# Hybrid trunk kernel: the loads of kept weight sums move to their place in the order of use

## The chip, the cores and the metric

The kernel runs on one NeuronCore of one Trainium2 chip. The metric is the device time of one execution in microseconds. Of three runs of the kernel before, the median is 1556.36 us, the lowest 1554.48 us and the highest 1556.77 us.

## The reference, cut to what matters

A decoder trunk of two layers works on 256 tokens of width 1024, all in float32. Each layer is a feed-forward block (FFN), a token mixer, and another FFN, so there are four FFNs; they are numbered 1 to 4 here, in order of time.

```python
def swiglu(x, w_in, w_out):
    gate, up = jnp.split(x @ w_in, 2, axis=-1)
    return (jax.nn.silu(gate) * up) @ w_out
...
    for l in range(DEPTH):
        h = h + 0.5 * swiglu(rms_norm(h, ffn1_norm[l]), ffn1_w_in[l], ffn1_w_out[l])
        u = rms_norm(h, mix_norm[l])
        ...
        h = h + merged @ w_out[l]
        h = h + 0.5 * swiglu(rms_norm(h, ffn2_norm[l]), ffn2_w_in[l], ffn2_w_out[l])
    return rms_norm(h, final_norm)
```

`w_in` of an FFN is 1024 x 5632 and `w_out` 2816 x 1024. The mixer (a state-space branch and a delta-rule branch) has its own large projections and runs between FFN 1 and 2, and between FFN 3 and 4.

## The kernel before, in words

**The weight stream.** All large weights come from one DRAM tensor, `wst`, cut into tiles of 128 x 1024 float32 (512 KB). A tile goes through three steps. `load` (L167) issues its DMA on SyncE's queue into one of five buffers `wraw` (`NRAW`). `prep` (L180) splits it in two: ScalarE writes the rounded half `whi`, VectorE the remainder `wlo = wraw - whi`; there are five buffers of each (`NSPL`). Then TensorE multiplies with both halves (three matmuls for one product: high by high, and the two cross terms). `take` (L206) is called by the consumer; it issues loads and splits ahead, five splits ahead of the consumer, and loads as far as the five buffers go.

**The FFN's plan.** The string `FFN` gives the order of an FFN's steps: `f` is the first token chunk (4 tiles), `c` a chunk of the input projection (2 tiles, `chan_chunk`), `A` and `B` are the two parts of a block product of the output projection, and `d` is one plain tile of the output projection:

```python
FFN = "f" + 8 * "c" + "A" + 4 * "c" + "A" + 4 * "c" + "A" + 2 * "c" + "A" + 2 * "c" + "BdBBBddddd"
```

Four pairs of output tiles are multiplied by a scheme with seven products in place of eight, which needs sums of weight blocks. Four of the products stand in `A` (the PSUM tiles `p`), three in `B` (the PSUM tiles `o`).

**The kept sum.** For each `A`/`B` pair one tile, named `wsum` in the profile, lives from before `A` until its `B`. There are four slots for it, `y0` to `y3`, each used once in an FFN (the mixer uses the same slots for other tiles). It is filled by a plain load of one block on SyncE's queue (kind `"y"` in `load`), and then a second block is added to it by an accumulating DMA on GpSimd's queue (kind `"+"`, `add_to`, L165), which waits until the first has landed. `plan_ffn` puts both into the stream two `c` steps ahead of their `A`. In `A`, `prep` splits the sum (step `q1`); VectorE adds one raw tile onto another (tile `wraw<-wraw` in the profile) and one raw tile onto the sum; step `q3` splits the sum again, and then `add_to` adds a third block by another accumulating DMA. Step `q6` in `B` splits it for the last time. So an FFN has four plain loads of `wsum` and eight accumulating DMAs.

**What sets the order.** The kernel is traced in program order and a scheduler then orders each engine's queue by priority and by what it believes is ready. `tc.issue_after(ins)` ties the instructions traced inside its block behind `ins` on the queue of `ins`; it adds no semaphore. A load into `wraw` needs a buffer that is given back by the splits, so it stays near its place in the stream. A load into a slot `y` needs only that the slot is free. SyncE's queue also carries the norm vectors `nw` (`norm_vec`, L216, tied behind the last load), the mixer's small parameters and its DRAM round trips. GpSimd's queue carries the accumulating DMAs, four accumulating DMAs onto `h` in each FFN (`join`, L421), and the small powers `zz` of the norms (L214).

**The end of an FFN.** After the last `B` come five `d` tiles, the residual `h`, the norm (`rms_chain`), and the first chunk of what follows. Each queue runs in its own order, and a queue whose head waits holds what stands behind it.

Of the kernel before, what the change touches and what calls it, by code (L numbers as in the profile page):

```python
# [52 lines left out]
def trunk_kernel(ctx, tc, x, wst, wsm, norms, lpar, rpar, cst, out):  # L53
    nc = tc.nc
# [103 lines left out]
    state = {"loaded": 0, "prepped": 0, "taken": 0, "last": None, "hold": False, "behind": {}, "late": {}, "first": 0}  # L158
    raws, halves = {}, {}

    def tile_of(i):
        return wst[i // 2, :, (i % 2) * 1024 :][:, 0:1024]

    def add_to(r, i):
        G.dma_start(out=r[:], in_=tile_of(i), accum_op=ALU.add)  # L165

    def load(j):  # L167
        kind, i = stream[j][:2]
        if kind == "+":
            add_to(raws[stream[j][2]], i)  # L170
            return
        if kind == "y":
            r = slots.tile([P, 1024], F32, tag=f"y{state['first']}", name="wsum")
            state["first"] = (state["first"] + 1) % 4
        else:
            r = wpool.tile([P, 1024], F32, tag="wraw", name="wraw", bufs=NRAW)
        state["last"] = nc.sync.dma_start(r[:], tile_of(i))
        raws[j] = r

    def prep(i):  # L180
# [25 lines left out]
    def take():  # L206
        j = state["taken"]
        state["taken"] = j + 1
        ahead("loaded", limit[min(j + NSPL, n_forms) - 1], load)
        ahead("prepped", min(j + 1 if state["hold"] else j + NSPL, n_forms), prep)  # L210
        return halves.pop(j)
# [15 lines left out]
    for t in range(2):  # L227
        for n in range(2):
            nc.sync.dma_start(
                h[:, t, n * 512 : (n + 1) * 512], x[t * P : (t + 1) * P, n * 512 : (n + 1) * 512]  # L230
            )
        if t == 0:
            nc.sync.dma_start(cs[:, 0:P], cst[:, 0:P])
            ahead("loaded", 4, load)
# [30 lines left out]
    def rstd_of(t):  # L265

        ss = small([P, 2], "ss")
        for n in range(2):
            junk = tmp2("junk")
            state["square"] = act(junk[:], h[:, t, n * 512 : (n + 1) * 512], AF.Square, scale=1.0 / 32.0, accum_out=ss[:, n : n + 1])  # L270
        z = small([P, 2], "zz")
        ts(z[:, 0:1], ss[:, 0:1], ss[:, 1:2], ALU.add, EPS, ALU.add)
        rsqrt(z[:, 1:2], z[:, 0:1], [P, 1])
        return z[:, 1:2]
# [978 lines left out]
    for t in range(2):  # L1253
# [5 lines left out]
        r = rstd_of(t)  # L1259
# [137 lines left out]
```

## Time and profile before

| what | value |
|---|---|
| median of three runs | 1556.36 us |
| profiled execution, its own time | 1555.2 us |
| its span, first to last instruction | 1553.4 us |
| mean granted TensorE clock | 0.997 |
| TensorE busy (matmul) | 1529.5 us, 98% |
| VectorE busy | 1210.0 us, 78% |
| ScalarE busy | 945.9 us, 61% |
| bytes moved by DMA | 322.50 MB, mean 208 GB/s |
| loads of `wsum` on SyncE's queue | 16 of 512 KB |
| accumulating DMAs onto `wsum` on GpSimd's queue | 32 of 512 KB |
| loads of `wraw` | 520 of 512 KB |

In the profile, PE is TensorE's matmuls, PEld its weight loads, DVE is VectorE, ACT is ScalarE, POOL is GpSimd, and SPq is SyncE's queue. A row of the timeline gives the start and the duration in us, the engine, the line, the operation, what it writes and reads, and in brackets the idle time of the engine before it with what ended that. A row of the stretches gives from and to, the length, then for each engine busy time and instructions, then the granted TensorE clock, the mean busy share of the 16 DMA engines, and GB/s. A matmul's duration is modelled and overlaps the next one; the step from start to start is its rate.

### The profile page before, as it was taken

The numbers are of one execution on the slowest core, as the hardware profiler recorded it, in microseconds if no ns is written. First come the engines' busy times: TensorE is split into PE (matmuls) and PEld (weight loads), VectorE is DVE, ScalarE is ACT, GpSimd is POOL, SyncE is SP. The second block draws the span as 40 slices with busy tenths as digits, with TensorE's granted clock in tenths as the row PEclk, the third lists the DMA queues.
The fourth block names the chain that finished last, engine by engine and source line by source line (L and its number), as shares of the span: only waits on it lengthen the run. The fifth ranks groups of instructions, "written<-read, shape, count | busy, mean of one in ns | idle before, by whom it ended". The sixth has DMA issues, their size and how long they took to land.

```text
span 1553.4 us, 29029 instructions
## 1 busy us (share of the span) xinstructions
PE 1529.5 (98%) x11458; PEld 1384.0 (89%) x11458; DVE 1210.0 (78%) x1840; ACT 945.9 (61%) x1534; POOL 100.7 (6%) x108
## 2 busy tenths in 40 slices
PE   8999999999999999999899999999999999999998
PEld 7999889999888888999689998899998888889996
DVE  6778768967899766878677787699579996677786
ACT  5555677765576545655455566676756665455564
POOL 0000110000000000000100011000000000000010
PEclk9999999999999999999999999999999999999999
DMA  8878775653564686678967787666446557856785
GB/s 292 262 244 261 229 224 165 190 158 109 192 202 163 212 239 200 180 241 248 313 199 209 219 258 231 206 187 187 124 126 213 178 165 223 245 179 199 226 250 156
DMA packets 103439, 322.50 MB, mean 208 GB/s; under 512 B 23350, under 2 KB 24326, under 8 KB 102279
## 3 DMA queue, kind: packets, MB, share of 16 engines
q1 hardware_dynamic: 96390, 299.68, 58.4%
q0 software_dynamic: 6912, 20.97, 8.0%
q8 instruction: 90, 1.47, 0.4%
q14 instruction: 47, 0.38, 0.1%
HBM read 314.50 MB, written 1.92 MB: 204 GB/s over the span
## 4 chain that ended last, share of the span: by engine, by line
PE 82%; DVE 6%; DMA 4%; issue 3%; ACT 3%; POOL 1%; SPq 0%; POOLq 0%; ACTq 0%; DVEq 0%
PE fc L332 9%; PE fc L326 9%; PE fc L331 9%; PE t L321 3%; PE t L322 3%; PE t L323 3%; DMA wraw<-in_wst_dram 3%; PE b L323 3%; PE b L321 3%; PE b L322 3%; PE o L323 2%; PE o L322 2%; PE o L321 2%; DVE wlo L70 2%; PE p L322 2%
## 5 line engine op out<-in xcount | busy, mean ns | idle before, releaser
L70 DVE TENSOR_TENSOR wlo<-wraw,whi 128x1024 fp32r<-128x1024 f32 x504 | 611.2, 1220 | 171.6 <-ACT whi L67 159.9
L67 ACT ACTIVATE whi<-wraw 128x1024 fp32r<-128x1024 f32 x504 | 527.7, 1058 | 275.8 <-PE fc L331 76.6
L332 PE MATMUL fc<-uW,wlo 128*128 128x256 f32 x1280 | 354.8, 277 | 0.0
L326 PE MATMUL fc<-uW,whi 128*128 128x256 f32 x1280 | 354.1, 277 | 0.0
L331 PE MATMUL fc<-uW,whi 128*128 128x256 f32 x1260 | 348.2, 276 | 0.0
L326 PEld LDWEIGHTS fc<-uW,whi 128*128 128x128 f32 x1280 | 240.3, 188 | 0.8
L332 PEld LDWEIGHTS fc<-uW,wlo 128*128 128x128 f32 x1280 | 240.5, 188 | 0.0
L331 PEld LDWEIGHTS fc<-uW,whi 128*128 128x128 f32 x1260 | 236.5, 188 | 0.8
L321 PE MATMUL t<-whi,uW 128*128 128x512 f32 x256 | 101.9, 399 | 0.0
L322 PE MATMUL t<-wlo,uW 128*128 128x512 f32 x256 | 100.9, 394 | 0.0
L323 PE MATMUL t<-whi,uW 128*128 128x512 f32 x256 | 100.6, 393 | 0.0
L321 PE MATMUL b<-whi,bh 128*128 128x512 f32 x192 | 76.2, 398 | 0.3 <-ACT bh L67 0.2
L322 PE MATMUL b<-wlo,bh 128*128 128x512 f32 x192 | 75.0, 390 | 0.0
L323 PE MATMUL b<-whi,bl 128*128 128x512 f32 x192 | 74.3, 394 | 0.3 <-DVE bl L70 0.3
L326 PE MATMUL xs<-uW,whi 128*128 128x256 f32 x256 | 72.7, 284 | 0.0
L332 PE MATMUL xs<-uW,wlo 128*128 128x256 f32 x256 | 71.3, 278 | 0.0
L331 PE MATMUL xs<-uW,whi 128*128 128x256 f32 x254 | 70.5, 277 | 0.0
L67 ACT ACTIVATE whi<-wsum 128x1024 fp32r<-128x1024 f32 x48 | 50.8, 1058 | 27.8 <-PE fc L331 23.3
L70 DVE TENSOR_TENSOR wlo<-wsum,whi 128x1024 fp32r<-128x1024 f32 x48 | 58.6, 1221 | 11.4 <-ACT whi L67 10.4
L322 PE MATMUL o<-wlo,gh 128*128 128x512 f32 x160 | 63.9, 399 | 2.5 <-DVE wlo L70 2.5
L321 PE MATMUL o<-whi,gh 128*128 128x512 f32 x160 | 63.9, 399 | 2.4 <-ACT whi L67 2.4
L165 POOL DMA_DIRECT2D wsum<-in_wst_dram x32 | 28.1, 878 | 582.3 <-DVE wlo L70 464.4
(332 smaller groups left out, 3430.4 us busy)
## 6 DMA issues: line engine op xcount, KB each, us to landing
wraw<-in_wst_dram SPq DMA_DIRECT2D x520, 512.0 KB, 5.0
wsum<-in_wst_dram POOLq DMA_DIRECT2D x32, 512.0 KB, 8.2
wsum<-in_wst_dram SPq DMA_DIRECT2D x16, 512.0 KB, 7.9
dc<-rdram SPq DMA_DIRECT2D x8, 1024.0 KB, 8.4
nw<-in_norms_dram SPq DMA_DIRECT2D x6, 512.0 KB, 6.8
h<-u POOLq DMA_DIRECT2D x12, 256.0 KB, 8.0
gb<-rdram SPq DMA_DIRECT2D x8, 256.0 KB, 5.7
h<-in_x_dram SPq DMA_DIRECT2D x4, 256.0 KB, 3.2
```

What stands on the lines that cost most here:

```text
L67: return A.activation(out=o, in_=i, func=func, **kw)
L70: return V.tensor_tensor(out=o, in0=a, in1=b, op=op)
L165: G.dma_start(out=r[:], in_=tile_of(i), accum_op=ALU.add)
L321: PE.matmul(ps, lh, rh, start=start, stop=False)
L322: PE.matmul(ps, lh, rl, start=False, stop=False)
L323: return PE.matmul(ps, ll, rh, start=False, stop=stop)
L326: PE.matmul(ps, wh, mh, start=start, stop=False)
L331: PE.matmul(ps, wh, ml, start=False, stop=False)
L332: PE.matmul(ps, wl, mh, start=False, stop=stop)
```

## The change

The load of a `wraw` tile is issued as before. The load of a `wsum` tile (any kind other than `"w"`) is now tied behind the load that was traced last, on SyncE's queue. The accumulating DMA waits for that load as before. The line numbers after L177 move by three.

```diff
         else:
             r = wpool.tile([P, 1024], F32, tag="wraw", name="wraw", bufs=NRAW)
-        state["last"] = nc.sync.dma_start(r[:], tile_of(i))
+        with ExitStack() as behind:
+            if kind != "w":
+                behind.enter_context(tc.issue_after(state["last"].ins))
+            state["last"] = nc.sync.dma_start(r[:], tile_of(i))
         raws[j] = r
```

The instructions of TensorE, VectorE and ScalarE are the same in the same order in both kernels. SyncE's and GpSimd's queues change.

SyncE's queue from the mixer of layer 0 to the mixer of layer 1, before (a `nw` is loaded near the start of an FFN, here of FFN 2 and then of FFN 3; the four `wsum` between them are those of FFN 3):

```order
L177 DMA wraw<-in_wst_dram 128x1024 x13
L219 DMA nw<-in_norms_dram 128x1024
L177 DMA wraw<-in_wst_dram 128x1024 x54
L177 DMA wsum<-in_wst_dram 128x1024
L177 DMA wraw<-in_wst_dram 128x1024 x3
L177 DMA wsum<-in_wst_dram 128x1024
L177 DMA wraw<-in_wst_dram 128x1024 x2
L177 DMA wsum<-in_wst_dram 128x1024
L177 DMA wraw<-in_wst_dram 128x1024 x2
L177 DMA wsum<-in_wst_dram 128x1024
L177 DMA wraw<-in_wst_dram 128x1024 x9
L219 DMA nw<-in_norms_dram 128x1024
```

The same place after, from the last `wsum` of FFN 2 on; the `nw` is the one near the start of FFN 3:

```order
L180 DMA wraw<-in_wst_dram 128x1024 x34
L222 DMA nw<-in_norms_dram 128x1024
L180 DMA wraw<-in_wst_dram 128x1024 x7
L180 DMA wsum<-in_wst_dram 128x1024
L180 DMA wraw<-in_wst_dram 128x1024 x11
L180 DMA wsum<-in_wst_dram 128x1024
L180 DMA wraw<-in_wst_dram 128x1024 x11
L180 DMA wsum<-in_wst_dram 128x1024
L180 DMA wraw<-in_wst_dram 128x1024 x7
L180 DMA wsum<-in_wst_dram 128x1024
L180 DMA wraw<-in_wst_dram 128x1024 x33
```

The four loads of FFN 3's sums stood among the last tiles of FFN 2, two or three tiles apart; they now stand inside FFN 3, with 11, 11 and 7 tiles between them. FFN 2's and FFN 4's four stood among the last tiles of the mixer ahead and move into their FFN in the same way, and FFN 1's four move from its first chunks to their places.

GpSimd's queue between the end of FFN 2 and the `A` parts of FFN 3, before (the number is that of the tile: 9035, 9398, 9735 and 9983 are the four sums in order):

```order
L427 DMA h_78<-u5_8636 128x512
L165 DMA wsum_9035<-in_wst_dram 128x1024
L165 DMA wsum_9398<-in_wst_dram 128x1024
L165 DMA wsum_9735<-in_wst_dram 128x1024
L165 DMA wsum_9983<-in_wst_dram 128x1024
L214 TENSOR_TENSOR zz_8797<-zz_8797,mhalf_96 128x1
L214 TENSOR_TENSOR zz_8833<-zz_8833,mhalf_96 128x1
L165 DMA wsum_9035<-in_wst_dram 128x1024
L165 DMA wsum_9398<-in_wst_dram 128x1024
L165 DMA wsum_9735<-in_wst_dram 128x1024
L165 DMA wsum_9983<-in_wst_dram 128x1024
```

The same place after:

```order
L430 DMA h_78<-u5_8636 128x512
L217 TENSOR_TENSOR zz_8797<-zz_8797,mhalf_96 128x1
L217 TENSOR_TENSOR zz_8833<-zz_8833,mhalf_96 128x1
L165 DMA wsum_9035<-in_wst_dram 128x1024
L165 DMA wsum_9398<-in_wst_dram 128x1024
L165 DMA wsum_9035<-in_wst_dram 128x1024
L165 DMA wsum_9735<-in_wst_dram 128x1024
L165 DMA wsum_9398<-in_wst_dram 128x1024
L165 DMA wsum_9983<-in_wst_dram 128x1024
L165 DMA wsum_9735<-in_wst_dram 128x1024
L165 DMA wsum_9983<-in_wst_dram 128x1024
```

The two powers of the norm now stand ahead of all eight accumulating DMAs. The first accumulation of a sum now stands directly ahead of the second accumulation of the sum before it.

## The prediction

> **What bounds the kernel now.** I read the page first: busy shares, the span in slices, and the DMA queues.
>
> ```profile
> span 1553.4 us, 29029 instructions
> PE   8999999999999999999899999999999999999998
> q1 hardware_dynamic: 96390, 299.68, 58.4%
> q0 software_dynamic: 6912, 20.97, 8.0%
> ```
>
> TensorE is busy in 90% or more of every slice but three: the first, the last, and one in the middle, around 740 to 780 us. So TensorE bounds the kernel, and a change of queue order can win only where TensorE waits. The queue rows give two prices. q1 carries plain loads: 58.4% of 1553.4 us for 299.68 MB is 1.6 us of all 16 engines for one 512 KB tile (0.524 MB). q0 carries GpSimd's accumulating DMAs: 8.0% for 20.97 MB is 3.1 us for one, twice as much.
>
> Second, the stretches of 25 us around that slice, beside the ends of FFN 3 and FFN 4:
>
> ```profile
> core 0: us, PE busy (x) PEld busy (x) DVE busy (x) ACT busy (x) POOL busy (x), PEclk, DMA share, GB/s
> 725.00:750.00 25.00, 25.00 (x160) 22.58 (x159) 20.26 (x23) 16.06 (x20) 5.23 (x6) 1.00 0.98 281
> 750.00:775.00 25.00, 20.24 (x71) 14.48 (x70) 12.04 (x11) 9.61 (x11) 2.59 (x3) 0.86 1.04 345
> 925.00:950.00 25.00, 25.00 (x126) 21.25 (x126) 22.08 (x23) 16.72 (x17) 3.49 (x4) 1.00 0.91 267
> 1500.00:1525.00 25.00, 25.00 (x160) 22.57 (x160) 20.00 (x22) 15.89 (x18) 3.50 (x4) 1.00 0.98 281
> ```
>
> From 750 to 775 us TensorE issued 71 matmuls, was idle for 4.76 us, and had a granted clock of 0.86, with the DMA engines full (1.04). At the same place in FFN 3 and FFN 4 it was never idle. This is the end of FFN 2, and the one FFN end of the three in whose tail the next FFN's sums are loaded. The timeline of TensorE there:
>
> ```profile
> 760.55 0.39 PE L323 MATMUL o<-whi,gl 128*128 128x512 f32 x1
> 761.10 0.49 PE L321 MATMUL o<-whi,gh 128*128 128x512 f32 x1 [0.16 <-ACT whi L67]
> 762.36 0.50 PE L322 MATMUL o<-wlo,gh 128*128 128x512 f32 x1 [0.77 <-DVE wlo L70]
> 768.65 0.80 PE L321 MATMUL o<-whi,gh 128*128 128x512 f32 x1 [1.73 <-ACT whi L67]
> 770.93 0.63 PE L321 MATMUL o<-whi,gh 128*128 128x512 f32 x1
> 774.35 0.63 PE L323 MATMUL o<-whi,gl 128*128 128x512 f32 x1
> 774.77 0.43 PE L321 MATMUL o<-whi,gh 128*128 128x512 f32 x1
> 775.51 0.39 PE L321 MATMUL o<-whi,gh 128*128 128x512 f32 x1
> 778.24 0.39 PE L321 MATMUL o<-whi,gh 128*128 128x512 f32 x1
> ```
>
> From 775.51 to 778.24 there are 12 steps: 0.2275 us each at full rate. From 770.93 to 774.35 there are 8 steps of 0.43 us: half rate. From 760.55 to 774.77 there are 22 matmuls; at full rate they take 5.0 us, they took 14.2 us. **The loss is 9.2 us**, part waiting for splits and part the half clock after it. The waits from 738 to 785 us and the two queues say who made the splits late:
>
> ```profile
> ACT whi L67 <- DMA wraw<-in_wst_dram: 9.5, 6, 2.7
> 739.05 0.33 SPq L177 DMA_DIRECT2D wsum<-in_wst_dram  x1
> 756.30 0.33 SPq L177 DMA_DIRECT2D wsum<-in_wst_dram  x1
> 747.50 0.87 POOL L165 DMA_DIRECT2D wsum<-in_wst_dram  x1 [3.89 <-DMA wsum<-in_wst_dram]
> 771.12 0.86 POOL L165 DMA_DIRECT2D wsum<-in_wst_dram  x1 [7.24 <-DMA wsum<-in_wst_dram]
> ```
>
> ScalarE waited six times, 9.5 us, for raw tiles to land. Between the first and the last of these rows lie four loads of `wsum` (739 to 756 us) and four accumulations (747 to 771 us), all for FFN 3, none needed before its first `A` (the row of 841.86 us below is that `A`'s own second accumulation). By the page's prices they are 4 x 1.6 + 4 x 3.1 = 18.8 us of full DMA engines.
>
> **The change part by part.** *(a) The end of FFN 2.* The 18.8 us of transfers leave the stretch from 739 to about 780 us. What stays is what FFN 4's end has (DMA share 0.98, TensorE 25.00 of 25). GpSimd's powers of the norm also no longer stand behind four accumulations. Nothing else in that stretch changes, so the whole loss should go: 9.2 us. Bounds: 0 (if FFN 2's own tiles were late by themselves) to 9.2. I take 9.2, since two undisturbed ends show no idle time.
>
> *(b) The `A` parts, in all four FFNs.* Here the change puts work in. Each of the four `A` parts of an FFN gets, in the tiles ahead of it, one load (1.6 us) and one accumulation (3.1 us) more: 4.7 us of DMA. The question is whether raw tiles get late. The closest place is FFN 2 and 3, between the first and third `A`:
>
> ```profile
> 841.86 0.89 POOL L165 DMA_DIRECT2D wsum<-in_wst_dram  x1 [54.15 <-DVE wlo L70]
> 869.24 0.86 POOL L165 DMA_DIRECT2D wsum<-in_wst_dram  x1 [26.48 <-DVE wlo L70]
> 654.68 0.89 POOL L165 DMA_DIRECT2D wsum<-in_wst_dram  x1 [54.39 <-DVE wlo L70]
> q0 software_dynamic: 119, 0.46, 77.5%
> q1 hardware_dynamic: 14, 0.06, 6.2%
> wraw<-in_wst_dram SPq DMA_DIRECT2D x3, 512.0 KB, 6.2
> 669.00:671.00 2.00, 2.00 (x20) 2.00 (x19) 2.00 (x5) 1.71 (x3) 0.00 (x0) 1.00 0.00 0
> 668.07 1.22 DVE L70 TENSOR_TENSOR wraw<-wraw 128x1024 f32<-128x1024 f32 x1 [2.60 <-DMA wraw<-in_wst_dram]
> 669.55 1.22 DVE L70 TENSOR_TENSOR wlo<-wraw,whi 128x1024 fp32r<-128x1024 f32 x1
> 672.02 1.22 DVE L70 TENSOR_TENSOR wlo<-wsum,whi 128x1024 fp32r<-128x1024 f32 x1
> 675.26 0.28 PE L326 MATMUL fc<-uW,whi 128*128 128x256 f32 x1
> 680.70 0.39 PE L321 MATMUL p<-whi,bsb 128*128 128x512 f32 x1
> ```
>
> The first two rows are the second accumulations of FFN 3's first and second `A`: one period is 27.4 us. It holds 11 raw tiles and one accumulation now, 11 x 1.6 + 3.1 = 20.7 us of DMA; after it is 25.4 us, still under 27.4. The next rows are FFN 2's first period. From 655.5 to 659.5 us (the two queue rows and the issues of raw tiles beside them) the accumulation almost alone holds the engines. VectorE then waits 2.60 us, until 668.07, for a raw tile that it adds onto another; this addition stands ahead of a split in its queue. At 669 to 671 us the DMA engines move nothing: the backlog is gone. The split behind the addition ends at 669.55 + 1.22 = 670.77, and TensorE needs it at 675.26: 4.5 us of room. The same place in FFN 3's second period is tighter:
>
> ```profile
> 884.04 1.22 DVE L70 TENSOR_TENSOR wraw<-wraw 128x1024 f32<-128x1024 f32 x1 [3.55 <-DMA wraw<-in_wst_dram]
> 885.51 1.22 DVE L70 TENSOR_TENSOR wlo<-wraw,whi 128x1024 fp32r<-128x1024 f32 x1
> 889.81 0.28 PE L326 MATMUL fc<-uW,whi 128*128 128x256 f32 x1
> ```
>
> The room is 889.81 - 886.73 = 3.1 us. After, the new accumulation stands right ahead of the old one on GpSimd's queue, so the raw tile is later by 3.1 us, or by 4.7 us if the new load finds no gap either. The stall at such a place lies between 0 and 4.7 - 3.1 = 1.6 us. There are two such places in each FFN, eight in all: 0 to 13 us. The row nearest is 669 to 671 us, empty: the new load falls into slack of this kind, and the room is 4.5 us in FFN 2. I take the low end, 1.0 us in all.
>
> *(c) Is the sum itself in time?* Two rows of the page's DMA part:
>
> ```profile
> wsum<-in_wst_dram POOLq DMA_DIRECT2D x32, 512.0 KB, 8.2
> wsum<-in_wst_dram SPq DMA_DIRECT2D x16, 512.0 KB, 7.9
> ```
>
> Load and accumulation take 7.9 + 8.2 = 16.1 us. A period has 12 splits; the load is issued about nine splits ahead of the sum's own, 9/12 of 27.4 = 20.5 us. Room of 4.4 us, and behind it the split of the sum in FFN 2 ends at 673.24 while TensorE wants it at 680.70, 7.5 us more. I cost it at nothing; the cover is these 12 us.
>
> *(d) The tail of the mixers and the start of FFN 1* lose the same eight transfers each. In the page's slices TensorE is at 9 there, so nothing is to be had; I take 0.
>
> *The sum.* The profiled execution took 1555.2 us: 1555.2 - 9.2 + 1.0 = 1547.0. The median of the runs is 1556.36, 1.2 us above it, so for a median I say 1548.2 us, 0.5% less.
>
> **Rivals.** *Slower: loads starve behind two accumulations in a row.* It is the mechanism of (b) at a higher price. For it: in the two queue rows q0 holds 77.5% of the engines and q1 6.2%, though SyncE issued three raw tiles in that time. If raw tiles get nothing while two accumulations run, and one of those needs some 4 us rather than 3.1 (655.5 to 659.5), the added delay is 4 + 1.6 = 5.6 us, beyond a room of 3.1 to 4.5 by 1.1 to 2.5 us; and after such waits the matmuls may run at half rate (8 steps of 0.43 us cost 1.6 us more). Eight places of about 1.8 + 1.6 us are 27 us: 1556.4 - 9.2 + 27 = 1574 us. It decides when a place costs over 9.2 / 8 = 1.15 us, a delay of 4.3 us where the room is 3.1. Against it: the backlog was gone by 669 us.
>
> By the Trainium skill, "DMA: Bandwidth & Descriptors", section "Queues, rings and completion order", each DMA engine takes turns between the queues that have work, a packet from each; then a raw tile is delayed by no more than the added transfer's own time, and this rival's price shrinks to that of (b). The two queue rows don't show turns, but tiles issued a moment before may not have reached the engines. By the skill's "TensorE: Matmul & The Clock Gate", section "Why this matters for your kernels", only idle gaps of more than about 3 us bring the low clock, and short waits in the `A` parts would cost themselves alone (1556.4 - 9.2 + 8 x 1.8 = 1561.6 us). The rows here disagree: the longest wait was 1.73 us, and half rate followed, so several short waits are enough.
>
> *No change: FFN 2's tail is late by itself.* Its own tiles and four accumulations onto `h` remain there, and DMA was already at 0.98 from 725 to 750 us. Then the loss stays: about 1556 us. Against it: FFN 4's end has 0.98 too, with no idle time. A mix of part of the gain given back in the `A` parts (6 to 12 us of the 0 to 13) ends here as well.
>
> **How the numbers follow.** Forecast, 1545 to 1553 us: 0.76. No change within 0.2% (3.1 us, about what a measurement of this kernel can tell): 0.11. Slower: 0.13. Low end: the lowest run, 1554.48, less 9.2 us is 1545.3. The high end takes in no change and the lower part of the slower rival: 1558.
>
> **What would show it.** Right: 750 to 775 us with TensorE at 25.00 and a clock of 1.00; the wait of ScalarE for `wraw` there gone; DMA share in the `A` periods up from about 20.7 / 27.4 = 0.76 to 25.4 / 27.4 = 0.93; VectorE's wait ahead of `wraw<-wraw` longer by 2 to 4 us and TensorE still full. Wrong: idle time of TensorE at `fc` or `p` rows in the second and third period of each FFN, or ScalarE waiting for the DMA of `wsum` ahead of the sum's split.

## The result and the profile after

The changed kernel takes 1563.83 us, the median of six runs (1562.49 to 1565.37). The kernel before takes 1556.57 us in the six runs beside them (1553.76 to 1559.66). The ratio is 1.0048 with a 95% interval of 1.0033 to 1.0062: slower by 7.3 us, where 8 us less had been forecast.

The page of the profile after, with the execution's span, TensorE's slices, the two DMA queues and VectorE's group for the additions of one raw tile onto another:

```profile
span 1563.3 us, 29046 instructions
PE   8999999999999999999999999999999999999997
q1 hardware_dynamic: 96390, 299.68, 57.2%
q0 software_dynamic: 6912, 20.97, 7.7%
L70 DVE TENSOR_TENSOR wraw<-wraw 128x1024 f32<-128x1024 f32 x16 | 19.6, 1226 | 71.2 <-DMA wraw<-in_wst_dram 71.2
```

The slice with an 8 in the middle is gone, and the bytes are the same. The group of additions has the same 16 instructions of the same length, but VectorE now waits 71.2 us ahead of them. The same group before:

```profile
L70 DVE TENSOR_TENSOR wraw<-wraw 128x1024 f32<-128x1024 f32 x16 | 19.6, 1225 | 39.0 <-DMA wraw<-in_wst_dram 39.0
```

Stretches of 25 us of the profile after: FFN 2 around its third `A`, the end of FFN 2, and the third `A` of FFN 3 and FFN 4:

```profile
core 0: us, PE busy (x) PEld busy (x) DVE busy (x) ACT busy (x) POOL busy (x), PEclk, DMA share, GB/s
700.00:725.00 25.00, 22.18 (x157) 21.03 (x156) 17.67 (x27) 12.56 (x18) 1.73 (x2) 0.93 0.87 252
750.00:775.00 25.00, 25.00 (x113) 20.70 (x112) 21.21 (x22) 15.71 (x18) 2.65 (x3) 1.00 0.94 282
875.00:900.00 25.00, 23.28 (x190) 22.22 (x189) 15.68 (x25) 11.42 (x17) 2.16 (x3) 1.00 0.86 244
1475.00:1500.00 25.00, 22.00 (x155) 20.85 (x154) 19.47 (x30) 12.29 (x18) 1.73 (x2) 0.93 0.84 252
```

The end of FFN 2 (second row) is full at a clock of 1.00: the gain came. But TensorE now stands still in three stretches in which it was full before. TensorE was busy for 25.00 us in all three rows of before; this is the first of them:

```profile
700.00:725.00 25.00, 25.00 (x196) 23.98 (x195) 21.91 (x32) 15.02 (x21) 0.86 (x1) 1.00 0.76 226
```

**Where the time went.** Both kernels issue the same matmuls in the same order, so the difference between the start of one matmul in two traces is the time lost up to it. I took it at eight matmuls, which start in the trace of before at 25, 225, 600, 750, 778, 1000, 1375 and 1525 us. After against before, in order: FFN 1 +4.1, the first mixer +0.7, FFN 2 +4.6, its end -9.3, FFN 3 +3.6, the second mixer +0.3, FFN 4 +5.6 us. With -0.4 us ahead of FFN 1 that is +9.2 us for this pair of executions. The end of FFN 2 gave 9.3 us, and the four FFNs together took 17.8 us. Most of it falls at one place of each FFN, the `fc` matmuls ahead of the third `A` and that `A` itself: 1.7, 4.75, 2.4 and 4.9 us, 13.8 us in all.

**What happens there, in FFN 2.** GpSimd's queue after (an `x2` row is two accumulations issued together), and the loads on SyncE's queue:

```profile
659.94 1.76 POOL L165 DMA_DIRECT2D wsum<-in_wst_dram  x2 [29.85 <-DMA wsum<-in_wst_dram]
692.92 1.76 POOL L165 DMA_DIRECT2D wsum<-in_wst_dram  x2 [31.22 <-DMA wsum<-in_wst_dram]
```

```profile
685.23 0.38 SPq L180 DMA_DIRECT2D wsum<-in_wst_dram  x1
686.95 11.68 SPq L180 DMA_DIRECT2D wraw<-in_wst_dram  x7
```

The pair at 692.92 us is the first accumulation of the third sum and, behind it, the second accumulation of the second sum. The first waits for its load, which was issued at 685.23 us. The second had been ready since 688.26 us, when the split of the second sum ended (687.04 + 1.22, in the next fence). It stood behind a waiting instruction for 4.7 us, and then both started together. Raw tiles were issued all through that time. The two queues from 697 to 704 us:

```profile
q0 software_dynamic: 249, 0.95, 69.1%
q1 hardware_dynamic: 234, 0.85, 32.7%
wsum<-in_wst_dram SPq DMA_DIRECT2D x1, 512.0 KB, 11.0
```

Accumulations (q0) hold 69.1% of the engines, plain loads (q1) 32.7%. A plain load issued here needs 11.0 us. VectorE, on the timeline and on the chain of waits (start, length, what):

```profile
687.04 1.22 DVE L70 TENSOR_TENSOR wlo<-wsum,whi 128x1024 fp32r<-128x1024 f32 x1
707.26 1.23 DVE L70 TENSOR_TENSOR wraw<-wraw 128x1024 f32<-128x1024 f32 x1 [8.98 <-DMA wraw<-in_wst_dram]
708.74 1.22 DVE L70 TENSOR_TENSOR wlo<-wraw,whi 128x1024 fp32r<-128x1024 f32 x1
710.08 1.22 DVE L70 TENSOR_TENSOR wlo<-wraw,whi 128x1024 fp32r<-128x1024 f32 x1
711.21 1.22 DVE L70 TENSOR_TENSOR wlo<-wsum,whi 128x1024 fp32r<-128x1024 f32 x1
```

```profile
697.21 10.03 DMA wraw<-in_wst_dram
707.24 0.02 issue
707.26 1.23 DVE wraw L70
708.49 0.33 DVE g L70
708.82 1.15 DVE wlo L70
```

The addition waits 8.98 us for a raw tile. The three splits behind it run one right after another, so they were held by the addition. TensorE needs the first of them:

```profile
710.01 0.38 PE L335 MATMUL fc<-uW,wlo 128*128 128x256 f32 x1 [2.82 <-DVE wlo L70]
712.09 0.41 PE L329 MATMUL fc<-uW,whi 128*128 128x256 f32 x1
714.23 0.41 PE L334 MATMUL fc<-uW,whi 128*128 128x256 f32 x1
```

It stands still for 2.82 us. From 712.09 to 714.23 us there are 10 steps of 0.21 us, twice the usual 0.113 us, so here too half rate follows the wait. The 4.75 us lost at this place are some 3 us of standing still and 1.7 us of slow steps. Half rate does not follow every such wait. At the same place of FFN 3 and FFN 4:

```profile
891.46 0.39 PE L335 MATMUL fc<-uW,wlo 128*128 128x256 f32 x1 [1.63 <-DVE wlo L70]
1481.88 0.38 PE L335 MATMUL fc<-uW,wlo 128*128 128x256 f32 x1 [3.00 <-DVE wlo L70]
```

After the 1.63 us the steps are full and the clock is 1.00 (stretch from 875 us above); after the 3.00 us it falls, to 0.93 on average from 1475 to 1500 us, as around the 2.82 us of FFN 2.

In the trace of before the same addition came in time:

```profile
695.92 1.22 DVE L70 TENSOR_TENSOR wraw<-wraw 128x1024 f32<-128x1024 f32 x1 [3.08 <-DMA wraw<-in_wst_dram]
```

From 695.92 to 707.26 us are 11.3 us. TensorE was 4.2 us later by then, so the addition is 7.1 us late against its consumer. The delay has two parts. This is the issue of the load that the addition waits for, before and after:

```profile
689.97 0.33 SPq L177 DMA_DIRECT2D wraw<-in_wst_dram  x1
697.21 0.33 SPq L180 DMA_DIRECT2D wraw<-in_wst_dram  x1
```

From its issue to the addition the tile takes 10.0 us in place of 5.9 us, 4.1 us more. And it is issued 7.2 us later, 3.0 us more than TensorE's 4.2 us. A load needs a buffer that earlier splits give back, and the splits of this FFN ran late since the addition ahead of the second `A`, which waited 5.9 us in place of 2.6 us; that this is the whole reason for the later issue is argued, not shown.

### The profile page after: what moved, and what is told of

Read it like the earlier page. It is cut to its first block, busy times and chain, and to the rows that moved or that the text cites. A ratio compares the mean times of both kernels' runs of the same rounds, so it can differ in the third digit from the quotient of the medians.

```text
span 1563.3 us, 29046 instructions
## 1 busy us (share of the span) xinstructions
PE 1534.5 (98%) x11458; PEld 1387.6 (89%) x11458; DVE 1206.9 (77%) x1840; ACT 939.4 (60%) x1534; POOL 100.4 (6%) x108
## 4 chain that ended last, share of the span: by engine, by line
PE 71%; DVE 12%; DMA 9%; ACT 4%; issue 3%; POOL 1%; SPq 1%; DVEq 0%; POOLq 0%; ACTq 0%
DMA wraw<-in_wst_dram 8%; PE fc L335 7%; PE fc L329 7%; PE fc L334 7%; DVE wlo L70 6%; PE t L324 3%; PE t L325 3%; PE t L326 3%; PE b L324 3%; PE b L326 3%; PE b L325 3%; PE o L326 2%; PE o L325 2%; ACT whi L67 2%; PE o L324 1%
## 5 line engine op out<-in xcount | busy, mean ns | idle before, releaser
L67 ACT ACTIVATE gh<-g 128x512 fp32r<-128x512 f32 x40 | 25.3, 633 | 95.8 <-DVE g L70 95.8
L70 DVE TENSOR_TENSOR wraw<-wraw 128x1024 f32<-128x1024 f32 x16 | 19.6, 1226 | 71.2 <-DMA wraw<-in_wst_dram 71.2
```

What stands on the lines that cost most here:

```text
L67: return A.activation(out=o, in_=i, func=func, **kw)
L70: return V.tensor_tensor(out=o, in0=a, in1=b, op=op)
```

## The experiments

The table has, for each run, the time, the ratio to the kernel before with its interval, the offsets of the profiled execution against that of before (as above, us lost), and VectorE's wait ahead of the 16 additions (39.0 us before). A dash means a single execution, without a ratio.

| run | us | ratio (95%) | FFN 1 | FFN 2 | its end | FFN 3 | FFN 4 | wait |
|---|---|---|---|---|---|---|---|---|
| after | 1563.83 | 1.0048 (1.0033 to 1.0062) | 4.1 | 4.6 | -9.3 | 3.6 | 5.6 | 71.2 |
| after, again | 1559.58 | - | 3.8 | 2.7 | -9.3 | 3.1 | 2.6 | 65.0 |
| only FFN 3 tied | 1553.73 | 0.9976 (0.9964 to 0.9987) | 0.0 | 0.0 | -9.3 | 2.0 | -0.2 | 46.3 |
| only FFN 3, early | 1549.66 | 0.9950 (0.9936 to 0.9963) | 4.2 | -0.2 | -9.3 | -0.1 | -0.2 | 42.4 |
| no second accumulation | 1547.08 | - | 0.0 | 0.0 | -9.3 | -0.2 | -0.2 | 37.4 |
| no first accumulation | 1546.86 | - | 0.0 | 0.0 | -9.3 | -0.2 | -0.2 | 35.0 |
| second accumulation later | 1548.77 | 0.9949 (0.9932 to 0.9965) | 0.0 | -0.1 | -7.9 | 0.0 | 2.6 | 45.2 |
| addition later | 1547.23 | 0.9938 (0.9925 to 0.9952) | 0.0 | -0.2 | -9.2 | 0.5 | 0.0 | 20.5 |
| before, addition later | 1554.72 | 0.9990 (0.9981 to 0.9999) | 0.5 | -0.2 | -2.2 | -0.1 | 0.0 | 4.4 |
| all early | 1546.82 | 0.9935 (0.9920 to 0.9950) | 0.0 | 0.0 | -9.3 | -0.1 | 0.0 | 37.9 |
| all early, addition later | 1547.52 | 0.9942 (0.9929 to 0.9956) | 0.2 | -0.2 | -9.3 | -0.3 | -0.2 | 1.9 |
| FFN 1 and 3 early, addition later | 1545.82 | 0.9930 (0.9918 to 0.9943) | 0.0 | -0.1 | -9.3 | -0.2 | 0.0 | 1.8 |

Most medians come from several executions, the offsets and waits always from one.

### One FFN alone: which half of the change gains, and which loses

The tie is kept for the four sums of FFN 3 alone (the counter `ys` counts loads of `wsum` in an FFN):

```diff
-            if kind != "w":
+            if kind != "w" and 8 < state["ys"] <= 12:
```

> The changed kernel with the tie for FFN 3's four loads alone; the loads of FFN 1, 2 and 4 are free as before the change. Theory (the tie gains at the end of FFN 2 and loses inside each FFN whose sums it moves in): the end of FFN 2 gains 9.3 us against before, FFN 3 loses 3 to 4 us as it did in the changed kernel, FFN 1, 2 and 4 lose nothing: 5 to 6 us faster than before, about 1551 us. Rival A (the loss is not tied to the place of the sums, but comes with any reordering): the total stays near the changed kernel's, 1560 us or more. Rival B (the gain at FFN 2's end needs FFN 2's own sums moved too): no gain there, about 1560 us.

The time was 1553.73 us, ratio 0.9976 (0.9964 to 0.9987). Its profiled execution was the fastest of its ten, 1548.11 us. There the end of FFN 2 gave its whole 9.3 us, FFN 3 lost 2.0 us, and the FFNs with the old order lost nothing. So the gain belongs to taking FFN 3's sums out of the end of FFN 2, and a loss goes with having them in the `A` periods. The median is 2.7 us above the expected 1551 us and 5.6 us above the profiled execution; where the other executions lost more was not profiled.

The second kernel keeps this and lets FFN 3's sums enter the stream among FFN 3's first `c` steps, one or two apart, so that the first accumulations are done before the first `A`:

```diff
-                spots.append(at - 2)
+                spots.append((3, 4, 6, 7)[len(spots)] if third else at - 2)
```

> As the run that ties FFN 3's loads alone, but with the four loads and first accumulations spread over the third to seventh input chunk of FFN 3, ahead of the first A, where no second accumulation runs. Theory (two accumulations of one period meet and make raw tiles late): the end of FFN 2 gains 9.3 us, and FFN 3 loses at most 1 us: 1547 to 1549 us, faster than both kernels. Rival (the amount of transfers that FFN 3 has to take in is what costs, wherever they stand): FFN 3 loses 3 to 5 us as before, 1551 to 1553 us.

The time was 1549.66 us, ratio 0.9950 (0.9936 to 0.9963): 4.1 us less than with the sums at their later place. In its profile FFN 3 loses nothing. FFN 1 lost 4.2 us in that execution, though nothing is changed there; it begins at an `fc` matmul at 64 us, not ahead of the third `A`. FFN 1 lost nothing in the run before, so this loss varies by execution, and what starts it is open.

### Which of the two accumulations

The third block is never added to a kept sum, in any FFN (16 accumulating DMAs fewer):

```diff
-        if kind == "q3":
-            add_to(r, js[1])
```

> The changed kernel without the sixteen second accumulations (the third block is never added to the kept sum, so the last product of each B works on incomplete sums). Theory (the loss is made by two accumulations meeting beside the raw tiles): the losses inside FFN 1 to 4 (18 us in all) fall to 2 us or less, and the run is at 1545 to 1548 us. Rival A (the first accumulation or the sum itself is late): the losses stay, 1560 us or more. Rival B (the amount alone counts, each transfer its share): with a third of the added and old transfers per period gone, about 6 to 9 us of the 18 stay, 1552 to 1556 us.

The other way round, the second block is never added, and the third is:

```diff
-            add_to(raws[stream[j][2]], i)
             return
```

> The changed kernel without the sixteen first accumulations (the kept sum lacks its second block); the plain loads stay where the change puts them. Theory (two accumulations meeting): the losses inside the FFNs fall to 2 us or less, 1545 to 1548 us, the same as without the second ones. Rival A (the plain load's new place makes the raw tiles late): the losses stay at 10 us or more, above 1556 us. Rival B (the amount): about 6 to 9 us stay.

A single execution each: 1547.08 and 1546.86 us. Either removal takes away the whole loss in all four FFNs and leaves the 9.3 us of gain. Their groups of additions, without the second and then without the first accumulation:

```profile
L70 DVE TENSOR_TENSOR wraw<-wraw 128x1024 f32<-128x1024 f32 x16 | 19.6, 1223 | 37.4 <-DMA wraw<-in_wst_dram 37.4
```

```profile
L70 DVE TENSOR_TENSOR wraw<-wraw 128x1024 f32<-128x1024 f32 x16 | 19.6, 1226 | 35.0 <-DMA wraw<-in_wst_dram 35.0
```

Both are a little below the 39.0 us of before. Neither accumulation is harmful by itself; the two in one period are. These runs do not tell apart whether it is their sum of bytes or that they start together.

### The same two accumulations, not together

The second accumulation is put six splits later, behind a small GpSimd copy that reads the newest split, so that it no longer starts with the first:

```diff
-            add_to(r, js[1])
+            state["pend"].append((i + 6, r, js[1]))
+        while state["pend"] and state["pend"][0][0] <= i:
+            _, held, block = state["pend"].pop(0)
+            gate = G.tensor_copy(out=mark[:], in_=f(lo[:, 0:1]))
+            with tc.issue_after(gate.ins):
+                add_to(held, block)
```

> The changed kernel with each second accumulation held back until six splits after its A (about 14 us), so that the same transfers stand in the same periods, but the two accumulations of a period run apart. Theory (they meet, and while both run raw tiles get a third of the engines): the losses inside the FFNs fall from 18 us to 5 us or less: 1547 to 1552 us. Rival (the amount of DMA in a period decides): the losses stay at 12 us or more: 1559 us and up.

The time was 1548.77 us, ratio 0.9949 (0.9932 to 0.9965). GpSimd's queue in FFN 2, and the stretch that had stood still:

```profile
657.74 0.87 POOL L165 DMA_DIRECT2D wsum<-in_wst_dram  x1 [31.14 <-PE p L332]
666.00 0.86 POOL L165 DMA_DIRECT2D wsum<-in_wst_dram  x1 [0.30 <-issue]
689.18 0.86 POOL L165 DMA_DIRECT2D wsum<-in_wst_dram  x1 [22.32 <-DMA wsum<-in_wst_dram]
695.22 0.86 POOL L165 DMA_DIRECT2D wsum<-in_wst_dram  x1 [0.33 <-issue]
```

```profile
700.00:725.00 25.00, 25.00 (x196) 23.85 (x195) 24.60 (x35) 14.49 (x21) 1.74 (x2) 1.00 0.85 257
```

The accumulations stand 8.3 and 6.0 us apart, nothing is removed, the DMA share is still 0.85, and TensorE is full. The load behind the addition (issued at 693.50 us) is 3.6 us late against TensorE, no less than in the changed kernel, but from its issue to the addition it takes 6.0 us, as in the kernel before; an addition 3.6 us late costs nothing there. So the slow transfer in FFN 2 goes with the pair starting together, and without it the bytes in the period make no loss. In FFN 4, 2.6 us stayed in this execution, ahead of the third `A`, with the accumulations 7.2 us apart; there the tile took 11.1 us. So keeping the two apart by some 7 us is not always enough, and the reason isn't known.

### The place of the addition on VectorE

Nothing of the DMA is touched. The addition of one raw tile onto another is tied behind the split that was traced last, so it no longer stands ahead of splits whose data are there:

```diff
-                tt(to, to, by, ALU.add)
+                with ExitStack() as lower:
+                    if kind == "q1":
+                        lower.enter_context(tc.issue_after(state["lo"].ins))
+                    tt(to, to, by, ALU.add)
...
-            tt(lo[:], r[:], f(hi[:]), ALU.subtract)
+            state["lo"] = tt(lo[:], r[:], f(hi[:]), ALU.subtract)
```

> The changed kernel with VectorE's addition of one raw tile onto another tied behind the split of the tile ahead, so that two splits no longer stand behind an addition that waits for a late raw tile. Theory (raw tiles late by some 7 us, and VectorE's fixed order turns that into a stall of TensorE): two splits and a product, 3 us, leave the wait; the loss at the worst places (FFN 2 and FFN 4, 4 to 5 us each) falls to about 1.5 us, all four FFNs together from 18 to 6 to 9 us: 1552 to 1556 us. Rival (TensorE waits for the raw tiles' own splits, not for those behind the addition): no gain, 1562 us or more.

The time was 1547.23 us, ratio 0.9938 (0.9925 to 0.9952). More came back than the 1552 to 1556 us expected: all of it. VectorE at the same place of FFN 2, and the stretches at the third `A` of FFN 2 and FFN 3:

```profile
697.15 1.23 DVE L70 TENSOR_TENSOR wlo<-wraw,whi 128x1024 fp32r<-128x1024 f32 x1 [2.20 <-ACT whi L67]
700.41 1.23 DVE L70 TENSOR_TENSOR wraw<-wraw 128x1024 f32<-128x1024 f32 x1 [2.03 <-DMA wraw<-in_wst_dram]
701.88 1.22 DVE L70 TENSOR_TENSOR wlo<-wsum,whi 128x1024 fp32r<-128x1024 f32 x1
```

```profile
700.00:725.00 25.00, 25.00 (x197) 24.01 (x196) 21.82 (x31) 14.87 (x21) 1.73 (x2) 1.00 0.84 258
875.00:900.00 25.00, 25.00 (x198) 24.05 (x198) 18.95 (x29) 12.66 (x20) 1.72 (x2) 1.00 0.91 289
```

The pair of accumulations is still issued together on GpSimd, and the addition still starts 4.5 us later than before (700.41 against 695.92 us). But a split now runs ahead of it, and TensorE is full with the DMA at 0.84 and 0.91. The raw tile's transfer is still slow (9.5 us from issue to addition), but its load is issued at 690.89 us, 0.8 us late against TensorE in place of 3.0 us. So the DMA engines' bandwidth was not what ran out. A late tile became a stall because VectorE's queue runs in order and a waiting addition stood at its head.

The same edit on the kernel before:

> The kernel before the change, with VectorE's addition tied behind the split ahead and nothing else moved. Theory: the loss at the end of FFN 2 (9.2 us) has nothing to do with that addition and stays; inside the FFNs the kernel before lost nothing, so there is little to win: within 2 us of the kernel before. Rival (the addition's place alone is what made the run with the later addition fast, and the loads' place matters little): 5 us or more faster than before.

The time was 1554.72 us, ratio 0.9990 (0.9981 to 0.9999). VectorE's wait ahead of the additions fell from 39.0 to 4.4 us, and TensorE gained next to nothing in the FFNs: before the change that wait was covered. At the end of FFN 2 the loss of before is still there, 2.2 us smaller in this execution:

```profile
750.00:775.00 25.00, 21.84 (x80) 15.93 (x80) 12.85 (x11) 10.48 (x12) 2.60 (x3) 0.86 1.04 345
```

So the edit by itself is worth 0.1%, and with the change it is worth 1.1% (1547.23 against 1563.83 us).

### Taking the first accumulations out of the `A` periods

All four FFNs put their sums into the stream among the first `c` steps; the tie stays, and VectorE is as in the changed kernel:

```diff
-                spots.append(at - 2)
+                spots.append((3, 4, 6, 7)[len(spots)])
```

> The changed kernel with all four loads of each FFN moved to the third to seventh input chunk, ahead of the first A, in all FFNs. Theory (first and second accumulations must not meet): the gain at the end of FFN 2 stays, 9.3 us, and the FFNs lose 0 to 1 us each: 1547 to 1551 us. Rival (any FFN that takes in its own eight transfers loses some 4 us): 1560 us or more.

The time was 1546.82 us, ratio 0.9935 (0.9920 to 0.9950). GpSimd's queue in FFN 2:

```profile
606.19 0.93 POOL L165 DMA_DIRECT2D wsum<-in_wst_dram  x1 [5.23 <-PE f L326]
614.03 0.87 POOL L165 DMA_DIRECT2D wsum<-in_wst_dram  x1 [6.91 <-PE fc L334]
624.34 0.86 POOL L165 DMA_DIRECT2D wsum<-in_wst_dram  x1 [9.44 <-DMA wsum<-in_wst_dram]
628.19 0.86 POOL L165 DMA_DIRECT2D wsum<-in_wst_dram  x1 [2.99 <-ACT whi L67]
655.35 0.86 POOL L165 DMA_DIRECT2D wsum<-in_wst_dram  x1 [26.29 <-DVE wlo L70]
682.72 0.86 POOL L165 DMA_DIRECT2D wsum<-in_wst_dram  x1 [26.50 <-DVE wlo L70]
```

The four first accumulations lie in the `c` steps, and each second one goes out when the split that it waits for ends, alone. The whole loss is gone with the same bytes and the same VectorE order.

Both edits together:

> All four FFNs' loads in the third to seventh input chunk, and VectorE's addition behind the split ahead. Theory: each of the two takes away the whole loss inside the FFNs, so together they add at most 1 us to either: 1545 to 1547 us. Rival (each takes away its own part): 1543 us or less.

The time was 1547.52 us, ratio 0.9942 (0.9929 to 0.9956), no better than either alone. Both cut the same chain of causes, so one cut is enough.

The last form ties only the sums of FFN 1 and FFN 3 and puts them early (steps 2, 4, 6, 7 and 3, 4, 6, 7), leaves FFN 2 and FFN 4 with the order of before, and has the addition later:

```diff
-            if kind != "w":
+            if kind != "w" and (state["ys"] <= 4 or 8 < state["ys"] <= 12):
```

> FFN 2's and FFN 4's loads free as before the change; FFN 1's and FFN 3's spread over their first input chunks; VectorE's addition behind the split ahead as in the run that moves the addition. Theory: the 9.3 us at the end of FFN 2 and nothing lost elsewhere; the spread in FFN 1 and the later addition take away what varied in FFN 1 (0 to 4 us from one execution to another): 1545 to 1549 us. Rival (FFN 1's variation comes from something else, at the start): 1549 to 1552 us, no better than FFN 3's spread alone.

The time was 1545.82 us (1545.04 to 1547.26), ratio 0.9930 (0.9918 to 0.9943). By the medians it is 18 us under the changed kernel, and its interval lies below the kernel before; from all sums early (1546.82 us) it isn't told apart.

### The changed kernel once more

> The changed kernel once more, unchanged, for a second profile. If the losses inside FFN 2, 3 and 4 (4.8, 3.9 and 5.5 us) are made by the order of the queues they come back at the same places with the same size within 1 us; FFN 1, whose cost varied from one execution to another in other runs, may differ by some 4 us.

One execution gave 1559.58 us. The places are the same: at the `fc` matmuls ahead of the third `A` and in that `A` TensorE lost 2.6, 2.2, 2.4 and 2.1 us, 9.3 of the 12.1 us in the FFNs. But the sizes are not: FFN 2 lost 1.9 us less than in the first profile and FFN 4 3.0 us less, where at most 1 us had been expected. In FFN 2 the pair was again issued together, at 693.14 us; TensorE then waited 1.43 us instead of 2.82 us:

```profile
708.99 0.39 PE L335 MATMUL fc<-uW,wlo 128*128 128x256 f32 x1 [1.43 <-DVE wlo L70]
```

The load behind the addition was issued 2.9 us late against TensorE, nearly as in the first profile, but took 8.8 us instead of 10.0 us. The four waits at these places were 1.26 to 1.77 us, and half rate followed none of them (the clock is 1.00 in all four stretches). The queue order doesn't fix the size of the loss, and what made the transfer shorter is open. The 7.3 us between the medians lie between the offsets of the two executions, 4.2 and 9.2 us.

## Why the prediction was wrong

**Step (a), the end of FFN 2, was right.** 9.2 us were forecast; 9.2 or 9.3 us came in each profile in which FFN 3's sums left that stretch but one (7.9 us, with the second accumulation later). The stretch from 750 to 775 us is full at a clock of 1.00.

**Step (b), the `A` parts, failed, and with it the sign.** It gave 1.0 us out of a range of 0 to 13 us; the two profiles show 17.8 and 12.1 us. The mechanism stood there in so many words: a raw tile later by the new accumulation, VectorE's addition waiting for it, two splits behind it, room of 3.1 to 4.5 us. What failed is the delay of the raw tile, the term that was set against the room. Three things were mis-sized.

- The delay was put at 3.1 us, or 4.7 us at most, the added transfers' own time. At the third `A` of FFN 2 it was 7.1 us. The slower transfer is 4.1 us of it, inside that bound. The other 3.0 us are the later issue of the load, for which the prediction had no term: the tiles ahead had come late too. At the same place of FFN 1, 3 and 4 the transfer was 3.0 to 3.6 us longer, and the issue about 0, 2 and 4 us later. On the transfer's side, the order that I had quoted shows the new accumulation directly ahead of the old one, and I counted only its transfer. I did not count that it waits for its load at the head of GpSimd's queue and holds the old one, ready for 4.7 us, until both start together with the raw tiles. The hold stands in the trace. That starting together matters in FFN 2 is shown by the run with the second accumulation later; what the hold costs by itself was not tried.
- The bound had no room for half rate after a wait, though the prediction had read just this at the end of FFN 2, and its slower rival had it. About 1.7 of the 4.75 us in FFN 2 are slow steps, and FFN 4 has the like; FFN 1 and FFN 3, with waits of 0.93 and 1.63 us, have none.
- The choice of the low end rested on the empty row from 669 to 671 us. That row shows free DMA engines after the backlog of one accumulation, in a period in which no second one came. It could not speak for two. That the period had DMA time left (25.4 of 27.4 us by the estimate) was beside the point: with the addition later TensorE is full in the same periods.

**The slower rival had the mechanism and too many places.** It named two accumulations in a row, raw tiles without bandwidth, half rate, eight places of 3.4 us, 1574 us, at a chance of 0.13. The profile shows four places of 3.4 us (13.8 / 4), or 2.3 us in the second profile, one in each FFN: the second addition of an FFN waits longer too, but TensorE loses next to nothing there. Its point of decision, a delay of 4.3 us, was passed. The Trainium skill's rule of turns between queues ("DMA: Bandwidth & Descriptors", "Queues, rings and completion order") had been put against it. The nearly equal numbers of packets, 249 and 234 side by side, agree with turns. The conclusion that I drew from it, that a raw tile loses no more than the added transfer's time, held for the tile's own transfer at this place (4.1 us against 4.7 us), but not for its delay (7.1 us), since the later issue comes on top. The Trainium skill's other rule ("TensorE: Matmul & The Clock Gate", "Why this matters for your kernels"), that only gaps of more than about 3 us bring the low clock, comes close for a single wait: half rate followed 2.82 and 3.00 us, and did not follow 1.77 us or less. At the end of FFN 2 before the change the longest wait was 1.73 us, but several stood close together. So the prediction's reading, that several short waits are enough, stands; for one such wait alone the rule was the better guide.

**Step (c), the sum in time, was right, with no room to spare.** 12 us of cover were counted. In FFN 2 the third sum's first accumulation landed at 702.41 us. ScalarE on its timeline rounds the sum 0.5 us later, right behind a raw tile, and waits for nothing:

```profile
702.93 1.04 ACT L67 ACTIVATE whi<-wsum 128x1024 fp32r<-128x1024 f32 x1
```

By then ScalarE had itself waited for that raw tile, so on time the cover would have been shorter still; in the run with the addition later TensorE is full all the same.

**Step (d), mixers and the start of FFN 1, at 0, was near enough.** The mixers lost 0.7 and 0.3 us. The kernel before with the addition later, in which no load moves, shows 1.1 and 0.4 us, so losses of this size come without the change. FFN 1's own loss ahead of its third `A` belongs to (b).

**The signs named beforehand.** Of those for a right forecast, the full stretch at 750 us came. The DMA share at the third `A` rose to 0.84 to 0.87, and to 0.84 and 0.91 where the periods are not lengthened (addition later), not to 0.93. VectorE's wait was to grow by 2 to 4 us with TensorE full: it grew by 1.6 to 4.4 us at each FFN's second addition and by 5.3 to 5.9 us at the third. Of those for a wrong one, idle time of TensorE at `fc` came, at the third `A`.

## What to carry to other kernels

When a change puts a DMA with a wait onto a queue, count what stands ready behind it: the held transfer goes out together with the new one, and loads meet both. A period's free DMA time does not tell whether one tile comes in time; ask which in-order queue waits for that tile and what ready work stands behind the wait, since moving that one instruction gained here as much as a better order of the transfers (1547.23 and 1546.82 us). Where the tiles ahead are late too, a load is also issued later (3.0 us here): count that beside its transfer. Half rate belongs into the price of a stall of nearly 3 us, or of several shorter ones close together; it followed no single wait of up to 1.77 us here.

## What the runs showed of the hardware

The price of sharing between the two kinds of queue was not expected. From 656 to 660 us of the trace of before an accumulation runs nearly alone, and from 663 to 668 us plain loads do:

```profile
656.00:660.00 4.00, 4.00 (x25) 3.49 (x24) 4.00 (x7) 3.55 (x4) 0.00 (x0) 1.00 0.94 153
663.00:668.00 5.00, 5.00 (x46) 5.00 (x45) 1.23 (x1) 2.40 (x3) 0.00 (x0) 1.00 1.00 394
```

Alone an accumulation moves 153 GB/s with the engines at 0.94, and plain loads 394 GB/s at 1.00. Side by side (697 to 704 us after) they move nearly equal bytes, 0.95 and 0.85 MB, in 249 and 234 packets, 259 GB/s together: one packet each in turn would look like this, and a packet of an accumulation takes about twice as long (69.1 / 249 against 32.7 / 234). So a plain load that meets accumulations gets about a third of the engines' time for as long as they last, here 32.7%, and lands after 10 to 11 us.
